# Low halves of part of the feed-forward weights formed by transfers that add the raw weight onto the negated high half

## The chip, the cores and the metric

The kernel runs on one core of one Trainium2 chip. The metric is the device time of one execution in microseconds. Engines are named as in the profile: PE multiplies matrices (PEld is its loading of weights), DVE is the vector engine, ACT the scalar engine, POOL the general-purpose one, and SP issues most transfers.

## The reference

The kernel computes a small encoder trunk for one sequence of 512 tokens with 1024 features, in float32. There are two layers, and each has four stages:

```
h = h + 0.5 * swiglu(rmsnorm(h, ffn1_norm[i]), ffn1_w_gu[i], ffn1_w_down[i])
h = h + mixer(rmsnorm(h, mix_norm[i]))       # layer 0: state-space scan, layer 1: neighbourhood attention
h = h + 0.5 * swiglu(rmsnorm(h, ffn2_norm[i]), ffn2_w_gu[i], ffn2_w_down[i])
h = h + sigmoid(rmsnorm(h, ple_norm[i]) @ ple_w_gate[i]) * rmsnorm(p[i] @ ple_w_proj[i], ple_post_norm[i])
```

`swiglu(x, w_gu, w_down)` splits `x @ w_gu` into a gate and an up half of 2816 columns each and returns `(silu(gate) * up) @ w_down`. The feed-forward stages are numbers 0, 2, 4 and 6 of the eight.

## The kernel before

**Two halves for every operand.** PE multiplies in a rounded 32-bit format, `float32r`. To come close to float32, each operand is split into a high half, rounded to that format, and a low half, the raw value minus the high half. A product takes three matmuls: high weight by high input, high weight by low input, low weight by high input (`gemm`, lines 282 to 292). Activations are split as they arise (`split`, line 314). Weights are split as they come in, by `split_raw` (line 228): ACT casts the raw tile into a tile `wh`, and DVE subtracts it from the raw tile into a tile `wl`.

**Units.** Weights come in units, tiles of 128 partitions by up to 1024 columns: eight blocks of 128 by 128 for a gate or an up row of tiles ("gu"), four or six blocks for a row of the down projection. The first units of a feed-forward stage, those before `chunks[0][1]`, are plain: 8 gate or up units in stages 2, 4 and 6, and 12 in stage 0. The rest of the gate and up projection is done in groups `p` of seven products instead of eight: `block(p, i)` multiplies a sum or difference of quarter matrices, in the order `TURN` (0, 3, 1, 5, 2, 4, 6). The tiles for the seven are made by DVE from four raw tiles (lines 252, 255, 257 and 263). Two of the four raw tiles lie in buffers `wr`, two in wide tiles `md`. Block 1 and block 5 share one tile: as soon as block 1 has been split, DVE overwrites it with block 5's values (line 263). `ffn_order` interleaves blocks with the down units ("dn") of the chunk before; after the last block come eight down units.

**The order around the split.** `plan` (line 152) lists everything that is to be prepared, in order: "u" a unit that is loaded and split, "g" four raw tiles taken as a group, "s" a sum of them, "o" a block whose tile is split. `prep_next` (line 238) does the next item of that list, and `top_up` (line 224) then issues loads from SP until three raw tiles in `wr` and two in `md` are waiting. `wr` has four buffers. `unit` (line 267) prepares until three units are ready and hands out the first. `wh` and `wl` have three buffers each, so the split of a unit waits until PE is done with the unit three places before it. The order within each engine's queue is that in which the code issues; a transfer waits in its issuing engine's queue until what it reads is written and what it overwrites is free.

**Around the stages.** `ffn` starts with the sum of squares for the norm (`SumSq`, line 335: squares on ACT, adds on POOL but for the last on DVE); while the first gate and up units run, DVE and ACT form the inputs for the blocks (`sums`, line 472). Results leave the accumulators through DVE and ACT: down products are added into `h` on DVE (line 599), block products by `whole` (line 535) on both. In the last down units of a stage, `Norm.prep` splits the new `h` and feeds POOL with squares to add. The first four units of stage 0 are loaded and split by hand (`begun`, lines 1437 to 1455), and `next(todo)` skips them in the list. POOL issues no transfer in this kernel.

Of the kernel before, what the change touches and what calls it, by code (L numbers as in the profile page):

```python
# [11 lines left out]
ALU = mybir.AluOpType  # L12
# [10 lines left out]
FIRST = ((0, 6), (6, 10), (10, 14), (14, 18), (18, 22))  # L23
OTHERS = ((0, 4), (4, 8), (8, 12), (12, 16), (16, 22))
# [28 lines left out]
def ffn_order(chunks):  # L53

    for f in range(chunks[0][1]):
        yield "plain", f
    yield "pair", 0, 0
    for c in range(1, len(chunks)):  # L60
        a, b = chunks[c]
        blocks = [(p, i) for p in range(a // 2, b // 2) for i in TURN]
        d = 2 if c == 1 else 0
        for n, (p, i) in enumerate(blocks):
            yield "block", p, i
            while d < KD and (d + 1) * len(blocks) <= KD * (n + 1):
                yield "down", c - 1, d
                d += 1
    yield "between",
    for d in range(KD):  # L70
        yield "down", len(chunks) - 1, d
# [3 lines left out]
def trunk(ctx, tc, A, out):  # L75
    nc = tc.nc
    v, s, g, te, sy = nc.vector, nc.scalar, nc.gpsimd, nc.tensor, nc.sync
# [13 lines left out]
    def nm(t):  # L91
        uid[0] += 1
        return f"{t}{uid[0]}"
# [55 lines left out]

    stop = A.get("stage", 4 * DEPTH)  # L150

    def plan():

        for i in range(stop):
            l, w = divmod(i, 4)
            if w in (0, 2):
                gu, gw, dn = [A[f"w_{x}{2 * l + w // 2}"] for x in ("gu", "gw", "dn")]
                chunks = FIRST if i == 0 else OTHERS  # L160
                plain = chunks[0][1]

                def ahead(p, i_):
                    if i_ == 0:
                        yield "g", [gw[p - plain // 2, x, y] for x, y in ((1, 0), (0, 0), (1, 1), (0, 1))]
                    yield "s", (p, i_)

                for what, *a in ffn_order(chunks):
                    if what == "plain":
                        for x in range(2):  # L170
                            yield "u", gu[a[0], x]
                            if 2 * a[0] + x == (6 if i == 0 else 3):
                                for n in range(3):
                                    yield from ahead(plain // 2, n)
                    elif what == "block":
                        yield "o", a
                        if a[1] in TURN[4:] and a[0] < NF // 2 - 1:
                            yield from ahead(a[0] + 1, TURN.index(a[1]) - 4)
                    elif what in ("down", "pair"):
                        b = chunks[a[0]]  # L180
                        for d in range(a[1], a[1] + 1 + (what == "pair")):
                            yield "u", dn[d, :, b[0] * P:b[1] * P]
                    elif w == 2:
                        for n in range(2):
                            yield "u", A["w_proj"][l, n]
            elif w == 3:
                for n in range(KD):
                    yield "u", A["w_gate"][l, n]
            elif l % 2 == 0:
                for n in range(65):  # L190
                    yield "u", A["w_in"][n]
                for x in range(2):
                    for d in range(KD):
                        yield "u", A["w_out"][d, :, x * 1024:(x + 1) * 1024]
            else:
                for n in range(24):
                    yield "u", A["w_qkv"][n]
                for d in range(KD):
                    yield "u", A["w_ao"][d]

    todo = list(plan())

    loads = [x for what, a in todo if what in "gu"
             for x in (zip(a, ("wr", "wr", "md", "md")) if what == "g" else [(a, "wr")])]
    todo = iter(todo)
    raws, ready, splits, group, blocks = [], [], [], [], {}
    waiting = {"wr": 0, "md": 0}

    def load_unit():
        src, tag = loads.pop(0)  # L210
        raw = wp.tile([P, 1024], F32, name=nm("wr"), tag="wr", bufs=4) if tag == "wr" else wide()
        n = src.shape[-1]
        sy.dma_start(out=raw[:, :n], in_=src)
        raws.append((raw, n, tag))
        waiting[tag] += 1

    def take():
        if not raws:
            load_unit()
        raw, n, tag = raws.pop(0)  # L220
        waiting[tag] -= 1
        return raw, n

    def top_up():
        while loads and waiting[loads[0][1]] < {"wr": 3, "md": 2}[loads[0][1]]:
            load_unit()

    def split_raw(raw, n):
        hi = wp.tile([P, 1024], F32R, name=nm("wh"), tag="wh", bufs=3)
        splits.append(s.copy(out=hi[:, :n], in_=raw[:, :n]))  # L230
        lo = wp.tile([P, 1024], F32R, name=nm("wl"), tag="wl", bufs=3)
        v.tensor_sub(out=lo[:, :n], in0=raw[:, :n], in1=hi[:, :n])  # L232
        ready.append((hi, lo))

    def wide():
        return md().rearrange("p a b -> p (a b)")

    def prep_next():
        item = next(todo, None)
        if item is None:  # L240
            return False
        what, a = item
        if what == "u":
            split_raw(*take())
        elif what == "g":
            group[:] = [take()[0] for _ in range(4)]
        elif what == "s":
            p, i = a
            a21, a11, a22, a12 = group
            if i == 0:  # L250
                blocks[p] = {0: a11, 2: a21, 3: wide(), 4: a12, 6: a22}
                v.tensor_add(out=blocks[p][3], in0=a21, in1=a22)
            elif i == 1:
                blocks[p][1] = blocks[p][5] = wide()
                v.tensor_sub(out=blocks[p][1], in0=blocks[p][3], in1=a11)
            else:
                v.tensor_sub(out=a21, in0=a11, in1=a21)
        else:
            p, i = a
            b = blocks[p]  # L260
            split_raw(b[i], 1024)
            if i == 1:
                v.tensor_sub(out=b[5], in0=b[4], in1=b[5])
        top_up()
        return True

    def unit(last=False):

        while (not last or not ready) and len(ready) < 3 and prep_next():
            pass  # L270
        return ready.pop(0)

    def ahead(norm):

        with tc.issue_after(norm.ss.last.ins):
            for _ in range(4):
                prep_next()
# [409 lines left out]
    def ssd(norm, nxt):  # L687
# [31 lines left out]
        for k in range(KD):  # L719
            t = t2()  # L720
            v.scalar_tensor_tensor(out=t, in0=hk[k], scalar=col(norm.gain + k), in1=R, op0=ALU.mult, op1=ALU.mult)
            xn.append(md(F32R))
            split(xn[k], t, None)
            if k == 5:
                prep_next()
# [709 lines left out]
    n = Norm(C_G1)  # L1435
# [57 lines left out]
    for i in range(stop):  # L1493
# [12 lines left out]
        n = m  # L1506
# [102 lines left out]
```

## Time and profile before

| | |
|---|---|
| median of three runs | 2292.43 us (2291.95 to 2293.34) |
| the profiled execution: its time | 2293.67 us |
| the profiled execution: its span, first to last instruction | 2291.9 us |
| granted TensorE clock | 0.999 |
| PE busy | 2273.0 us |
| DVE busy | 1847.5 us |
| ACT busy | 1287.3 us |
| POOL busy | 324.6 us |
| DMA packets | 281.57 MB |

The span leaves out what lies before the first and after the last instruction; here that is 1.8 us. A row of the groups gives line, engine, operation, output and inputs, shapes and count, then the busy time and the mean of one in ns, then the engine's idle time ahead of these instructions and what ended it. A row of the chain gives its start and length in microseconds. A row of the timeline gives start and length, then the instruction. A row of the waits gives the total, the count and the longest. A row of the transfers gives size and median from issue to landing.

### The profile page before, as it was taken

To read this page: it belongs to the slowest core of one execution; us is meant where nothing else is said; L and a number is where in the kernel's file an instruction comes from. 1 tells how busy PE (TensorE), PEld (TensorE's weight loads), DVE (VectorE), ACT (ScalarE), POOL (GpSimd) and SP (SyncE) were. 2 spreads that over 40 slices of the span, in tenths; PEclk is the share of its full clock that TensorE was granted. 3 is DMA by queue.
4 is the path that set the end of the run, shared out by engine and by line. 5 is a ranking of instruction groups with operands and counts; after the bars stand their busy time and mean duration, and the time that the engine had idled before them with its cause. 6 is when DMAs were issued, how large, how long until landed. Compare 5 with 4: busy or idle time off the path is not lost.

```text
span 2291.9 us, 33293 instructions
## 1 busy us (share of the span) xinstructions
PE 2273.0 (99%) x12458; PEld 1949.9 (85%) x12458; DVE 1847.5 (81%) x2729; ACT 1287.3 (56%) x2332; POOL 324.6 (14%) x261
## 2 busy tenths in 40 slices
PE   9999999999999999999999999999999999999999
PEld 7888888888888888888888878888877888888887
DVE  8878878888788959988885898888577859888866
ACT  6444445777677765544456554445546755444463
POOL 0000001345555641000003100000110010000020
PEclk9999999999999999999999999999999999999999
DMA  5323323444444643233223233232457732333232
GB/s 193 111 91 103 105 83 138 151 153 139 147 138 150 186 165 120 101 103 106 97 76 108 101 103 105 93 106 74 168 173 219 230 114 89 105 110 106 79 98 77
DMA packets 105090, 281.57 MB, mean 123 GB/s; under 512 B 13008, under 2 KB 13904, under 8 KB 104928
## 3 DMA queue, kind: packets, MB, share of 16 engines
q1 hardware_dynamic: 104640, 279.30, 37.0%
q8 instruction: 98, 1.61, 0.3%
q14 instruction: 64, 0.52, 0.1%
q10 hardware_dynamic: 288, 0.14, 0.0%
HBM read 259.70 MB, written 13.40 MB: 119 GB/s over the span
## 4 chain that ended last, share of the span: by engine, by line
PE 88%; DVE 8%; ACT 1%; issue 1%; DMA 1%; POOL 0%; SPq 0%; DVEq 0%; POOLq 0%; ACTq 0%
PE ps L518 29%; PE ps L287 18%; PE ps L291 18%; PE ps L290 17%; DVE wl L232 2%; PE ps L929 1%; PE ps L970 1%; DVE md L317 1%; PE ps L950 1%; PE ps L885 1%; PE ps L874 1%; PE ps L1367 1%; PE ps L1313 1%; PE ps L1356 0%; DVE t L790 0%
## 5 line engine op out<-in xcount | busy, mean ns | idle before, releaser
L287 PE MATMUL ps<-md,wh 128*128 128x512 f32 (+1 forms) x2032 | 797.6, 393 | 1.5 <-DVE t L790 1.5
L291 PE MATMUL ps<-md,wl 128*128 128x512 f32 (+1 forms) x2032 | 791.6, 390 | 3.7 <-DVE wl L232 3.7
L290 PE MATMUL ps<-md,wh 128*128 128x512 f32 (+1 forms) x2032 | 790.5, 389 | 0.8 <-DVE md L320 0.8
L230 ACT CAST wh<-wr 128x1024 fp32r<-128x1024 f32 (+2 forms) x395 | 352.3, 894 | 399.5 <-PE ps L290 181.0
L232 DVE TENSOR_TENSOR wl<-wr,wh 128x1024 fp32r<-128x1024 f32 (+2 forms) x395 | 417.4, 1059 | 115.3 <-ACT wh L230 113.3
L291 PEld LDWEIGHTS ps<-md,wl 128*128 128x128 f32 x2032 | 381.9, 188 | 86.1 <-DVE wl L232 4.8
L287 PEld LDWEIGHTS ps<-md,wh 128*128 128x128 f32 x2032 | 382.1, 188 | 78.1 <-ACT wh L230 2.1
L290 PEld LDWEIGHTS ps<-md,wh 128*128 128x128 f32 x2032 | 382.2, 188 | 74.8 <-DVE md L320 1.1
L518 PE MATMUL ps<-md,wh 128*128 128x256 f32 (+1 forms) x1610 | 366.4, 308 | 0.0
L518 PE MATMUL ps<-sc,wh 128*128 128x512 f32 (+1 forms) x1190 | 362.2, 357 | 0.4
L345 POOL TENSOR_TENSOR sq<-sq,sq 128x512 f32<-128x512 f32 x71 | 101.1, 1424 | 1627.9 <-ACT sq L341 642.2
L230 ACT CAST wh<-md 128x1024 fp32r<-128x1024 f32 x175 | 184.2, 1053 | 204.1 <-PE ps L518 170.0
L518 PEld LDWEIGHTS ps<-md,wh 128*128 128x128 f32 x1610 | 261.1, 189 | 20.1
L518 PE MATMUL ps<-md,wl 128*128 128x256 f32 x980 | 277.0, 283 | 1.1 <-DVE wl L232 1.1
L518 PE MATMUL ps<-sc,wl 128*128 128x256 f32 x980 | 276.4, 282 | 0.5 <-DVE wl L232 0.5
L232 DVE TENSOR_TENSOR wl<-md,wh 128x1024 fp32r<-128x1024 f32 x175 | 214.2, 1225 | 65.2 <-ACT wh L230 61.0
L518 PEld LDWEIGHTS ps<-sc,wh 128*128 128x128 f32 x1190 | 209.8, 188 | 35.7 <-DVE t L542 1.0
L518 PEld LDWEIGHTS ps<-sc,wl 128*128 128x128 f32 x980 | 184.9, 189 | 6.0 <-DVE wl L232 1.7
L518 PEld LDWEIGHTS ps<-md,wl 128*128 128x128 f32 x980 | 185.4, 189 | 2.9 <-DVE wl L232 2.9
L599 DVE SCALAR_TENSOR_TENSOR hs<-ps,hs 128x512 f32<-128x512 f32 x152 | 104.6, 688 | 72.8 <-PE ps L291 72.3
L790 DVE SCALAR_TENSOR_TENSOR t<-ps,ccw,t 128x510 f32<-128x510 f32 (+1 forms) x180 | 134.0, 745 | 10.7 <-ACT t L786 7.9
L542 DVE TENSOR_TENSOR t<-ps,t 128x256 f32<-128x256 f32 x280 | 116.4, 421 | 7.2 <-ACT t L541 5.0
(216 smaller groups left out, 2454.5 us busy)
## 6 DMA issues: line engine op xcount, KB each, us to landing
wr<-in_w_gw_dram SPq DMA_DIRECT2D x70, 512.0 KB, 3.2
md<-in_w_gw_dram SPq DMA_DIRECT2D x70, 512.0 KB, 3.6
wr<-in_w_in_dram SPq DMA_DIRECT2D x65, 512.0 KB, 3.3
wr<-in_w_dn_dram SPq DMA_DIRECT2D x128, 256.0 KB, 2.6
wr<-in_w_gu_dram SPq DMA_DIRECT2D x32, 512.0 KB, 3.4
hs<-crow SPq DMA_DIRECT2D x64, 256.0 KB, 3.6
wr<-in_w_dn_dram SPq DMA_DIRECT2D x32, 384.0 KB, 3.0
wr<-in_w_qkv_dram SPq DMA_DIRECT2D x24, 512.0 KB, 3.8
```

Of the source, the lines that this page charges most:

```text
L230: splits.append(s.copy(out=hi[:, :n], in_=raw[:, :n]))
L232: v.tensor_sub(out=lo[:, :n], in0=raw[:, :n], in1=hi[:, :n])
L287: m = te.matmul(out=pt, lhsT=hi[:, sl], rhs=part(xp, 0, cols), start=first and k == 0, stop=False)
L290: te.matmul(out=pt, lhsT=hi[:, sl], rhs=part(xp, 1, cols), start=False, stop=False)
L291: gemm.last = te.matmul(out=pt, lhsT=lo[:, sl], rhs=part(xp, 0, cols), start=False, stop=last and k == n - 1)
L317: split.low = v.tensor_sub(out=dst[:, 1, :], in0=src, in1=dst[:, 0, :])
L345: (v if fast else g).tensor_add(out=self.acc, in0=self.acc, in1=q)
L518: mm = lambda o, w, x, st, sp_: te.matmul(out=o, lhsT=w, rhs=x, start=opens and st, stop=sp_, skip_group_check=not opens)
L542: v.tensor_add(out=o, in0=pt[j][:, :HT], in1=o)
L599: v.scalar_tensor_tensor(out=h[d], in0=pt, scalar=0.5, in1=h[d], op0=ALU.mult, op1=ALU.add)
L790: v.scalar_tensor_tensor(out=a[:, lo:hi], in0=src[:, lo + o:hi + o], scalar=w(j), in1=a[:, lo:hi], op0=ALU.mult, op1=ALU.add)
L874: te.transpose(out=pt[:, cs(i)], in_=src[:, cs(c)], identity=ident)
```

## The change

The list of things to prepare is built stage by stage, so that the units of each feed-forward stage can be counted. In these stages the plain units, and from then on every second unit (the second, the fourth and so on), are marked. For a marked unit, ACT casts the high half as before, and then writes the negated high half into the tile `wl`; POOL then issues a transfer that reads the raw tile and adds it onto `wl`. DVE's subtraction is left out for these units. All other units are split as before.

```diff
-    todo = list(plan())
+    todo, by_dma = [], set()
+    for i in range(stop):
+        here = len(todo)
+        todo += plan([i])
+        if i % 2 == 0:
+            units = [n for n in range(here, len(todo)) if todo[n][0] in "uo"]
+            plain = 2 * (OTHERS if i else FIRST)[0][1]
+            by_dma.update(units[:plain] + units[plain + 1::2])
...
-    todo = iter(todo)
+    todo = ((n in by_dma, *item) for n, item in enumerate(todo))
...
-    def split_raw(raw, n):
+    def split_raw(raw, n, by_dma=False):
         hi = wp.tile([P, 1024], F32R, name=nm("wh"), tag="wh", bufs=3)
         splits.append(s.copy(out=hi[:, :n], in_=raw[:, :n]))
         lo = wp.tile([P, 1024], F32R, name=nm("wl"), tag="wl", bufs=3)
-        v.tensor_sub(out=lo[:, :n], in0=raw[:, :n], in1=hi[:, :n])
+        if by_dma:
+            s.mul(out=lo[:, :n], in_=hi[:, :n], mul=-1.0)
+            g.dma_start(out=lo[:, :n], in_=raw[:, :n], accum_op=ALU.add)
+        else:
+            v.tensor_sub(out=lo[:, :n], in0=raw[:, :n], in1=hi[:, :n])
         ready.append((hi, lo))
...
-        what, a = item
+        dma, what, a = item
         if what == "u":
-            split_raw(*take())
+            split_raw(*take(), dma)
...
-            split_raw(b[i], 1024)
+            split_raw(b[i], 1024, dma)
```

More of the change, by code (lines that the diff above doesn't have):

```diff
@@ L150, in trunk, with plan @@
     stop = A.get("stage", 4 * DEPTH)
-    def plan():
-        for i in range(stop):
+    def plan(stages):
+        for i in stages:
             l, w = divmod(i, 4)
```

## The prediction

> **What bounds the kernel now.** I read the page's totals first, then the chain, then the busy time in the stretches where most of the changed weights are used, then who waited for whom.
>
> ```profile
> span 2291.9 us, 33293 instructions
> PE 2273.0 (99%) x12458; PEld 1949.9 (85%) x12458; DVE 1847.5 (81%) x2729; ACT 1287.3 (56%) x2332; POOL 324.6 (14%) x261
> ...
> PE 88%; DVE 8%; ACT 1%; issue 1%; DMA 1%; POOL 0%; SPq 0%; DVEq 0%; POOLq 0%; ACTq 0%
> ```
>
> PE is without work for 2291.9 - 2273.0 = 18.9 us in all. The 8% of DVE in the chain is no reserve of that size: the chain follows DVE while PE still works off earlier units. The block-and-down part of each of the four feed-forward stages shows it more sharply:
>
> ```profile
> core 0: us, PE busy (x) PEld busy (x) DVE busy (x) ACT busy (x) POOL busy (x), PEclk, DMA share, GB/s
> 82.00:330.00 248.00, 248.00 (x1478) 220.32 (x1477) 195.91 (x268) 115.48 (x173) 0.00 (x0) 1.00 0.28 90
> 950.00:1195.00 245.00, 245.00 (x1480) 218.20 (x1479) 205.13 (x284) 116.94 (x178) 0.00 (x0) 1.00 0.29 98
> 1350.00:1590.00 240.00, 239.50 (x1444) 212.89 (x1443) 202.53 (x278) 115.95 (x175) 0.00 (x0) 1.00 0.29 95
> 1990.00:2230.00 240.00, 240.00 (x1394) 211.45 (x1393) 189.17 (x260) 124.91 (x191) 13.98 (x10) 1.00 0.30 96
> sum 973.00, PE 972.50 PEld 862.86 DVE 792.75 ACT 473.28 POOL 13.98; mean PE 243.13 PEld 215.71 DVE 198.19 ACT 118.32 POOL 3.49
> ```
>
> In 973 us PE idles 0.5 us. DVE is busy for 81% of that time and hides behind PE completely. What PE waited for the low halves is small in the whole run:
>
> ```profile
> PEld ps L291 <- DVE wl L232: 4.8, 3, 3.1
> PEld ps L518 <- DVE wl L232: 4.6, 12, 0.6
> ```
>
> So relieving DVE can bring at most 4.8 + 4.6 = 9.4 us. The question is what the longer way of making a low half does to PE.
>
> **How much cover there is.** `wh` and `wl` have three buffers each, and `unit()` prepares up to three units ahead. A unit's split can start when the unit three before it is finished, and must be done when the two units between are finished. The cover is the length of two units.
>
> ```profile
> 203.14 2.81 PE ps L518 x16
> 205.95 0.24 PE ps L287
> ...
> 208.74 5.69 PE ps L518 x40
> ```
>
> These rows of the chain run without a gap, and give the lengths: a block takes 2.81 us, a down unit over four blocks (twelve matmuls) 208.74 - 205.95 = 2.79, so the cover is **5.6 us**. A gate or up unit has 24 of the same matmuls, 5.58 us; its cover is 11.2. What uses it today:
>
> ```profile
> 203.00 1.05 ACT L230 CAST wh<-wr 128x1024 fp32r<-128x1024 f32 x1 [1.00 <-ACT t L554]
> ...
> 204.08 1.23 DVE L232 TENSOR_TENSOR wl<-wr,wh 128x1024 fp32r<-128x1024 f32 x1 [0.21 <-ACT wh L230]
> ```
>
> The cast starts at 203.00, as the preceding down unit ends, and the low half is there at 205.31: 2.3 of 5.6 us.
>
> **The change part by part.** Counting in program order, 235 low halves go the new way: 121 blocks, 64 down units of 512 columns, 16 of 768, 2 `w_proj` units, and 32 gate and up units; all but the last 32 alternate with units split by DVE.
>
> ```profile
> L230 ACT CAST wh<-wr 128x1024 fp32r<-128x1024 f32 x235 | 245.7, 1049 | 208.6 <-PE ps L290 119.9 <-PE ps L518 33.1 <-issue 27.5
> L230 ACT CAST wh<-md 128x1024 fp32r<-128x1024 f32 x175 | 184.2, 1053 | 204.1 <-PE ps L518 170.0 <-PE ps L290 13.0 <-DVE md L263 11.5
> L230 ACT CAST wh<-wr 128x512 fp32r<-128x512 f32 x128 | 79.8, 623 | 149.5 <-PE ps L518 66.3 <-PE ps L290 45.3 <-issue 32.7
> L230 ACT CAST wh<-wr 128x768 fp32r<-128x768 f32 x32 | 26.8, 837 | 41.4 <-issue 18.8 <-PE ps L290 15.8 <-PE ps L518 6.1
> ...
> L232 DVE TENSOR_TENSOR wl<-md,wh 128x1024 fp32r<-128x1024 f32 x175 | 214.2, 1225 | 65.2 <-ACT wh L230 61.0
> L232 DVE TENSOR_TENSOR wl<-wr,wh 128x512 fp32r<-128x512 f32 x128 | 87.4, 684 | 4.1 <-ACT wh L230 3.7
> L232 DVE TENSOR_TENSOR wl<-wr,wh 128x768 fp32r<-128x768 f32 x32 | 31.6, 990 | 16.7 <-ACT wh L230 16.4
> ```
>
> Removed from DVE: 155 x 1.225 + 64 x 0.684 + 16 x 0.990 = 250 us, nearly all behind a busy PE, so worth nothing by itself. Added to ACT: a multiplication of the same shape as the cast, which I price like it: 155 x 1.05 + 64 x 0.62 + 16 x 0.84 = 216 us. Of these some 182 fall on the alternating parts, where ACT would rise from 473 to 655 of 973 us; it stays unbound, and the copies queued behind a multiplication are late by at most 1.05 us, less than a unit. But both casts of a unit now stand one behind the other on the way to its low half.
>
> Then comes a transfer that POOL issues and that adds. The trace has neither kind. The nearest rows:
>
> ```profile
> wr<-in_w_gw_dram SPq DMA_DIRECT2D x70, 512.0 KB, 3.2
> md<-in_w_gw_dram SPq DMA_DIRECT2D x70, 512.0 KB, 3.6
> ...
> wr<-in_w_dn_dram SPq DMA_DIRECT2D x128, 256.0 KB, 2.6
> ...
> md<-md SPq DMA_DIRECT2D x8, 256.0 KB, 6.3
> ```
>
> ```profile
> L345 POOL TENSOR_TENSOR sq<-sq,sq x71: 1286/1302/2275, 339.9 to 2241.0; 128x512 f32<-128x512 f32 x71
> ```
>
> Lower end for a block (512 KB): the plain load, 3.2 us. Upper end: the slow row from SBUF to SBUF, 6.3 us for 256 KB, doubled: 12.6. I take the loads as the nearer rows, as they move whole rows of these very tiles: 3.4 us (between 3.2 and 3.6), plus one more stream of 512 KB, since the adding transfer reads its destination too. The step from 256 to 512 KB costs 3.4 - 2.6 = 0.8, so two such steps, 1.6. For POOL's issuing I take the 1.3 us of its median instruction, as an estimate. Together 6.3 us for a block, and 2.6 + 0.8 + 1.3 = 4.7 for a down unit of 512 columns.
>
> A block's low half then takes 1.05 + 1.05 + 0.05 for the hand-overs (the cast above ended at 204.05, DVE began at 204.08), so 2.15, + 6.3 = 8.45 us against 5.6: it is late by **2.85 us**. A down unit takes 0.62 + 0.62 + 0.05 + 4.7 = 6.0, late by 0.4. The 768-column units stand mostly among their like, with 8 us of cover. Gate and up units have 11.2 and are not late.
>
> How often is it paid? While PE waits for one late unit, the buffers of the unit behind it are free already, so the next unit by transfer starts that much earlier: of two late blocks in a row the second is on time, and a down unit after a late block always is. In the program's order the 121 blocks form 50 runs between down units, of 1 to 6 blocks; a run of r pays (r+1)/2, rounded down, which gives 16 + 19 + 19 + 19 = 73 times. 73 x 2.85 = **208 us**.
>
> Smaller edits. At block 1, DVE overwrites the very tile that the transfer reads (line 263):
>
> ```profile
> L263 DVE TENSOR_TENSOR md<-md,md 128x1024 f32<-128x1024 f32 x35 | 42.6, 1218 | 0.0
> ```
>
> Nine of these now wait for a transfer, with DVE's evacuations and the next low half queued behind; DVE is released as PE starts block 1, and has 1.22 + 0.84 + 1.23 = 3.3 us to do against the block's 2.81: about 0.5 x 9 = 5 us. The raw buffer comes free later too, and SP's loads queue behind it:
>
> ```profile
> 196.06 0.33 SPq L213 DMA_DIRECT2D wr<-in_w_dn_dram  x1
> ...
> 208.55 0.62 ACT L230 CAST wh<-wr 128x512 fp32r<-128x512 f32 x1 [1.30 <-PE ps L290]
> ```
>
> Counting loads and casts in order, these are one unit: landed at 198.7, it lay ready for 9.9 us, more than the 6 us by which a release moves; nothing. Past POOL's queue: it has nothing in three of the four stretches, and in the fourth ten adds, in the last down units; each can be held by one issue. Nothing. Against the 5 us stand some 5 of the 9.4 that PE waits for low halves today. The sum is 208; with the profiled execution's 2293.7 us it makes 2501.7, and as that lies 1.2 above the median of the runs, **2500**.
>
> One rule of the Trainium skill prices a transfer of this path: "DMA: Bandwidth & Descriptors", section "Anatomy of one DMA — SWDGE (gpsimd) path", fits about 2.0 us plus the bytes over 436 GB/s for transfers that GpSimd issues, without a word on adding ones. For 512 KB that is an estimated 3.2 us, beside the 3.2 to 3.6 of the loads here; by it the sum would be zero, which is the second rival below. No run here shows such a transfer yet.
>
> **The rivals.** *A, the forecast (0.62)*: the transfer takes 4.5 to 8 us for a block, late by 1.05 to 4.55, 73 times: 77 to 332 us, 2369 to 2624 us, which is its own range. *B, a far slower transfer (0.20)*: more than 8 us, because adding runs at a fraction of the copying rate, or because issuing is held up by DVE. For it speak the 6.3 us row above and this one:
>
> ```profile
> L982 DVE TENSOR_TENSOR sc<-sc,md x16: 693/1480/1516, 471.9 to 837.6; 128x512 f32<-128x512 f32 x16
> ```
>
> The same instruction takes 0.69 or 1.48 us, and the long ones run beside POOL's adds; DVE and POOL can get in each other's way, and DVE is 81% busy here. The Trainium skill ("SBUF — State Buffer", "Who interferes with whom") says the same of a DVE instruction with two SBUF inputs beside a POOL instruction that reads SBUF. At 10 us a block is late by 6.55: 478 us, 2770. Against it: SP's loads take their 3.2 to 3.6 us beside the same busy DVE, and POOL has nothing else to do in these stretches. *C, hidden (0.09)*: up to 5.6 - 2.15 = 3.45 us for a block nothing is late. The plain load of the same size speaks for it, the second stream and POOL's issue against: 2292. *D, faster (0.09)*, the other side: again at most 3.45 us, and DVE, free of 250 us, no longer lets PE wait where the gate and up units start; most of the 9.4 us: about 2285.
>
> **How the numbers follow.** This kernel's measurement can tell about 0.2% (4.6 us) from no change. Slower by more: A and B, 0.82; within: C, 0.09; faster: D, 0.09. The predicted time is A's, 2500. The range leaves out D and the upper half of B: 2290 (no lateness) to 2790 (a transfer of some 10.2 us).
>
> **What would show it.** Right: PE's busy share falls to about 91%, with gaps of some 3 us, 70 to 80 of them in the four stretches, ahead of block matmuls (L518) and released by a transfer into `wl`; few ahead of down units; hardly any in gate and up units; DVE down by about 250 us and ACT up by about 216; the transfers' median from issue to landing, POOL's issue included, near 6.3 and 4.7 us. B shows as 9 us and more, with gaps at gate and up units too. Wrong: block transfers under 3.45 us and a full PE (C, D); or gaps that end with DVE or with a load, which would put the loss on line 263 or on the raw buffers.

## The result and the profile after

The changed kernel takes 2538.68 us (median of four runs, 2532.43 to 2545.55), before 2292.89 us: a ratio of 1.1076 (95% interval 1.1062 to 1.109), 246 us slower. The profiled execution took 2532.43 us. In the changed kernel the lines have moved by 11: the matmuls of the blocks are L529, those of the other units L298, L301 and L302, line 263 is now L274. In `split_raw`, L237 is the cast, L240 the negation on ACT, L241 the transfer and L243 DVE's subtraction.

From the page of the changed kernel (totals, queues, chain, transfers):

```profile
span 2530.6 us, 33976 instructions
...
PE 2345.1 (93%) x12458; PEld 1970.4 (78%) x12458; DVE 1632.9 (65%) x2494; ACT 1480.8 (59%) x2567; POOL 527.6 (21%) x496
...
q0 software_dynamic: 33840, 104.35, 22.2%
...
PE 57%; DMA 19%; issue 17%; DVE 4%; ACT 2%; POOL 0%; SPq 0%; POOLq 0%; DVEq 0%; ACTq 0%
...
wl<-md POOLq DMA_DIRECT2D x83, 512.0 KB, 5.0
wl<-wr POOLq DMA_DIRECT2D x72, 512.0 KB, 4.7
...
wl<-wr POOLq DMA_DIRECT2D x64, 256.0 KB, 3.2
```

The 235 transfers are there (33840 packets on a queue of their own), and they now make 19% of the chain. A block's takes 4.7 to 5.0 us from issue to landing, a down unit's 3.2. PE is without work for 2530.6 - 2345.1 = 185.5 us, 166.6 more than before. Whom PE waited for, in the changed kernel (total, count, longest):

```profile
PE ps L529 <- DMA wl<-md: 94.3, 62, 3.0
PE ps L302 <- DMA wl<-wr: 55.1, 39, 5.1
PE ps L529 <- DMA wl<-wr: 12.4, 7, 2.6
PE ps L529 <- DVE t L553: 7.4, 4, 1.9
```

Transfers into `wl` end 108 waits of 161.8 us: 69 of them (106.7 us) at blocks, the 39 of L302 (55.1 us) at the other units. By the trace, 11 of these 39 (18.0 us) lie in the gate and up units at the stage starts, and nearly all others in down units. The first of the four stretches, from the busy times by window, and the timeline of one block by transfer in it:

```profile
82.00:330.00 248.00, 220.33 (x1233) 187.06 (x1232) 133.59 (x188) 125.89 (x179) 30.43 (x35) 0.98 0.58 146
```

```profile
104.74 1.05 ACT L237 CAST wh<-md 128x1024 fp32r<-128x1024 f32 x1 [1.35 <-PE ps L529]
105.82 1.06 ACT L240 ACTIVATE wl<-wh 128x1024 fp32r<-128x1024 f32 x1
...
107.29 0.87 POOL L241 DMA_DIRECT2D wl<-md  x1 [5.68 <-ACT wl L240]
```

PE worked 220.33 of 248 us, where it had worked all 248. After the cast and the negation end at 106.88, POOL begins 0.41 us later, and its issuing takes 0.87.

Weight loads come late too. Who waited for them, before and then in the changed kernel:

```profile
ACT wh L230 <- DMA wr<-in_w_gu_dram: 2.8, 3, 1.0
ACT wh L230 <- DMA wr<-in_w_dn_dram: 1.0, 2, 0.6
DVE md L252 <- DMA wr<-in_w_gw_dram: 0.3, 1, 0.3
```

```profile
DVE md L266 <- DMA wr<-in_w_gw_dram: 39.6, 23, 4.8
DVE md L263 <- DMA wr<-in_w_gw_dram: 33.7, 16, 7.0
ACT wh L237 <- DMA wr<-in_w_gu_dram: 32.2, 13, 5.6
ACT wh L237 <- DMA wr<-in_w_dn_dram: 11.9, 6, 3.0
DVE md L263 <- DMA md<-in_w_gw_dram: 9.2, 3, 4.9
```

That is 126.6 us instead of 4.1 for the weights of the feed-forward stages. These are waits of ACT and DVE, not of PE; how much of them reaches PE is a question for the experiments.

PE's busy time has also grown, by 2345.1 - 2273.0 = 72.1 us, with the same 12458 matmuls. The mean granted clock is 0.984 instead of 0.999: (1 - 0.984) x 2530.6 - (1 - 0.999) x 2291.9 = **38 us** went to a slower clock. Windows around a wait of 1.78 us (for DVE, as it happens), then PE's timeline there:

```profile
87.00:90.00 3.00, 1.47 (x10) 1.11 (x8) 3.00 (x5) 1.13 (x3) 0.86 (x1) 1.00 0.25 51
90.00:92.00 2.00, 1.76 (x6) 1.46 (x7) 1.66 (x3) 0.64 (x1) 0.00 (x0) 0.62 0.94 186
92.00:94.00 2.00, 2.00 (x9) 1.71 (x8) 0.00 (x0) 1.46 (x2) 0.10 (x1) 0.53 0.00 0
94.00:97.00 3.00, 3.00 (x26) 2.91 (x25) 0.00 (x0) 1.05 (x1) 0.76 (x1) 1.00 0.64 128
```

```profile
90.24 0.63 PE L529 MATMUL ps<-sc,wh 128*128 128x512 f32 x1 [1.78 <-DVE t L553]
...
94.00 0.40 PE L529 MATMUL ps<-sc,wh 128*128 128x512 f32 x1
```

After the wait the clock is at about half for some 3.4 us (the shortfalls of the second and third window together), and the same matmul takes 0.63 instead of 0.40 us.

### The profile page after: what moved, and what is told of

It is laid out like the page before. It is cut to its first block, busy times and chain, and to the rows that moved or that the text cites. A ratio compares the mean times of both kernels' runs of the same rounds, so it can differ in the third digit from the quotient of the medians.

```text
span 2530.6 us, 33976 instructions
## 1 busy us (share of the span) xinstructions
PE 2345.1 (93%) x12458; PEld 1970.4 (78%) x12458; DVE 1632.9 (65%) x2494; ACT 1480.8 (59%) x2567; POOL 527.6 (21%) x496
## 3 DMA queue, kind: packets, MB, share of 16 engines
q0 software_dynamic: 33840, 104.35, 22.2%
## 4 chain that ended last, share of the span: by engine, by line
PE 57%; DMA 19%; issue 17%; DVE 4%; ACT 2%; POOL 0%; SPq 0%; POOLq 0%; DVEq 0%; ACTq 0%
PE ps L529 14%; PE ps L302 13%; PE ps L301 13%; PE ps L298 13%; DMA wl<-md 8%; DMA wl<-wr 6%; DMA wr<-in_w_gu_dram 1%; DMA wr<-in_w_dn_dram 1%; DMA wr<-in_w_gw_dram 1%; PE ps L940 1%; PE ps L981 1%; DVE wl L243 1%; PE ps L896 1%; PE ps L961 1%; PE ps L885 1%
## 5 line engine op out<-in xcount | busy, mean ns | idle before, releaser
L302 PE MATMUL ps<-md,wl 128*128 128x512 f32 (+1 forms) x2032 | 802.8, 395 | 55.8 <-DMA wl<-wr 55.1
L298 PE MATMUL ps<-md,wh 128*128 128x512 f32 (+1 forms) x2032 | 804.4, 396 | 1.4 <-DVE t L801 1.3
L301 PE MATMUL ps<-md,wh 128*128 128x512 f32 (+1 forms) x2032 | 797.4, 392 | 0.8 <-DVE md L331 0.8
L237 ACT CAST wh<-wr 128x1024 fp32r<-128x1024 f32 (+2 forms) x395 | 351.6, 891 | 376.7 <-PE ps L301 217.0
L302 PEld LDWEIGHTS ps<-md,wl 128*128 128x128 f32 x2032 | 385.8, 190 | 155.9 <-DMA wl<-wr 74.1
L298 PEld LDWEIGHTS ps<-md,wh 128*128 128x128 f32 x2032 | 385.8, 190 | 79.2 <-ACT wh L237 4.1
L301 PEld LDWEIGHTS ps<-md,wh 128*128 128x128 f32 x2032 | 386.1, 190 | 75.4 <-DVE md L331 1.1
L529 PE MATMUL ps<-sc,wh 128*128 128x512 f32 (+1 forms) x1190 | 372.7, 364 | 7.4 <-DVE t L553 7.4
L529 PE MATMUL ps<-md,wh 128*128 128x256 f32 (+1 forms) x1610 | 375.8, 313 | 4.0 <-ACT wh L237 3.8
L529 PE MATMUL ps<-sc,wl 128*128 128x256 f32 x980 | 285.7, 292 | 70.6 <-DMA wl<-md 58.1
L237 ACT CAST wh<-md 128x1024 fp32r<-128x1024 f32 x175 | 183.7, 1050 | 265.5 <-PE ps L529 215.1
L243 DVE TENSOR_TENSOR wl<-wr,wh 128x1024 fp32r<-128x1024 f32 (+2 forms) x243 | 270.6, 1115 | 103.2 <-ACT wh L237 96.1
L529 PE MATMUL ps<-md,wl 128*128 128x256 f32 x980 | 283.7, 290 | 36.6 <-DMA wl<-md 36.2
L241 POOL DMA_DIRECT2D wl<-wr x152 | 132.3, 870 | 833.6 <-ACT wl L240 586.7
L529 PEld LDWEIGHTS ps<-md,wh 128*128 128x128 f32 x1610 | 267.2, 194 | 27.6 <-ACT wh L237 7.7
L529 PEld LDWEIGHTS ps<-sc,wl 128*128 128x128 f32 x980 | 190.7, 195 | 91.9 <-DMA wl<-md 71.2
L529 PEld LDWEIGHTS ps<-sc,wh 128*128 128x128 f32 x1190 | 215.6, 194 | 41.5 <-DVE t L553 8.8
L529 PEld LDWEIGHTS ps<-md,wl 128*128 128x128 f32 x980 | 190.0, 194 | 52.8 <-DMA wl<-md 48.8
L240 ACT ACTIVATE wl<-wh 128x1024 fp32r<-128x1024 f32 (+2 forms) x235 | 217.3, 926 | 3.2
L241 POOL DMA_DIRECT2D wl<-md x83 | 72.3, 871 | 527.4 <-ACT wl L240 255.5
```

Of the source, the lines that this page charges most:

```text
L240: s.mul(out=lo[:, :n], in_=hi[:, :n], mul=-1.0)
L241: g.dma_start(out=lo[:, :n], in_=raw[:, :n], accum_op=ALU.add)
L298: m = te.matmul(out=pt, lhsT=hi[:, sl], rhs=part(xp, 0, cols), start=first and k == 0, stop=False)
L301: te.matmul(out=pt, lhsT=hi[:, sl], rhs=part(xp, 1, cols), start=False, stop=False)
L302: gemm.last = te.matmul(out=pt, lhsT=lo[:, sl], rhs=part(xp, 0, cols), start=False, stop=last and k == n - 1)
L529: mm = lambda o, w, x, st, sp_: te.matmul(out=o, lhsT=w, rhs=x, start=opens and st, stop=sp_, skip_group_check=not opens)
```

## The experiments

Each run has its own time before, on the same chip: 2292 to 2295 us. The change itself spread over 13 us in four runs, so single runs are not read closer than that.

| run | what it does | us |
|---|---|---|
| the change | | 2538.68 |
| e1 | plain gate and up units only | 2317.34 (ratio 1.0114, 1.0097 to 1.013) |
| e10 | blocks only | 2466.88 |
| e12 | down units only | 2323.88 (ratio 1.0132, 1.0115 to 1.0149) |
| e7 | transfer copies, doesn't add | 2359.79 |
| e3 | negated half first | 2498.09 |
| e8 | four buffers, four ahead | 2411.30 |
| e11 | e3, e8 and five raw buffers | 2346.69 |
| e6 | five raw buffers | 2516.87 |
| e2 | second pass on ACT, DVE adds | 2305.56 |
| e4 | transfers beside, from the raw tiles | 2387.00 |
| e5 | transfers beside, from the masks | 2743.43 |

The theory is the prediction's: a low half by transfer comes later than its two units of cover, and PE waits for it. The main rival is that the transfers cost by what they hold up elsewhere: loads, raw buffers, POOL, ACT.

**Which units pay: e1, e10, e12.** The edit is the list of marked units; e10 and e12 differ in the letter.

```diff
-            by_dma.update(units[:plain] + units[plain + 1::2])
+            by_dma.update(units[:plain])                                               # e1
+            by_dma.update(n for n in units[plain + 1::2] if todo[n][0] == "o")         # e10
+            by_dma.update(n for n in units[plain + 1::2] if todo[n][0] == "u")         # e9, e12
```

e1 was expected:

> Only the plain gate and up units (32 of the 235) are split by transfer; the alternating ones go back to DVE. Lateness theory (a low half by transfer takes about 8 us from the release of its buffers, and only units with less than that as cover are late): gate and up units have 11.2 us of cover, so no loss; between 2283 and 2297 us, likeliest 2290. Rival, every transfer costs wherever it stands (traffic, POOL, ACT): 32/235 of the 246 us, so about 2326.

It lost 25 us, nearer the rival's 34 than nothing, so the gate and up units are not free. Its waits and its queues at the start of stage 2 show why (waits; POOL's, then SP's timeline):

```profile
PE ps L302 <- DMA wl<-wr: 18.5, 10, 5.0
...
ACT wh L237 <- DMA wr<-in_w_gu_dram: 32.1, 15, 5.6
```

```profile
894.88 0.87 POOL L241 DMA_DIRECT2D wl<-wr  x1 [1.91 <-ACT wl L240]
...
903.13 0.33 SPq L220 DMA_DIRECT2D wr<-in_w_gu_dram  x1
```

The same load of before:

```profile
894.17 0.33 SPq L213 DMA_DIRECT2D wr<-in_w_gu_dram  x1
```

The raw buffer comes free only when the transfer has read it, and by the trace this one, issued at 894.88 beside several loads, landed 8.2 us later. So the load starts at 903.13 instead of 894.17, ACT waits for the raw weight, and its transfer starts late. Ten waits of PE follow. It is the chain of raw buffer, load, cast and transfer that is too long here, not the cover of `wl`: two of the four `wr` buffers are held by the raw tiles of the coming group.

> Of the alternating units only the 121 blocks are split by transfer; down, w_proj and plain units go back to DVE. Lateness theory: a block needs 1.05 + 1.05 + 0.4 + 4.9 = 7.4 us against 5.6, late by 1.8, for 73 to 121 blocks (fewer where one gives the next a head start), so 131 to 218 us and the slower clock after the long waits on top: 2425 to 2530. Rival, every transfer costs 1.05 us: 2420 at the most, and as much more than the run with the down units alone as 39 more transfers cost, 41 us.

The blocks alone cost 174 us, 1.44 each, within the theory's range.

> Of the alternating units only the down units (and the two w_proj units) are split by transfer, 82 in all; blocks and plain units go back to DVE. Lateness theory: a down unit of 512 columns needs 0.62 + 0.62 + 0.4 (hand-over to POOL) + 3.2 = 4.9 us against 5.6 of cover and is not late by itself: 2293 to 2315 us. Rival, every transfer costs about the same (246 us over 235, 1.05 each): 2375.

e9 gave 4584.86 us. In that execution every matmul was slow, in the stages without a changed unit too, with nothing for PE to wait for:

```profile
L298 PE MATMUL ps<-md,wh 128*128 128x512 f32 (+1 forms) x2032 | 1374.4, 677 | 0.0
```

The kernel before took 2292.64 us on the same chip. The run says nothing about the edit, and the same kernel was run again:

> The kernel of the run before that splits only the down and w_proj units by transfer, once more, since there every matmul of the whole run took twice its time (4584.86 us), in the stages without a changed unit too. Lateness theory as before: 2293 to 2315 us. Rival, every transfer costs about the same: 2375.

29 us for 82 transfers, 0.36 each: a little over the theory's range and far from one price for all. PE waited 20 times for a transfer:

```profile
PE ps L302 <- DMA wl<-wr: 20.9, 20, 2.6
```

The three parts, 25 + 174 + 29 = 228 of 246 us, nearly add up, and the blocks carry three quarters of it.

**The transfer's length: e7.**

```diff
-            g.dma_start(out=lo[:, :n], in_=raw[:, :n], accum_op=ALU.add)
+            g.dma_start(out=lo[:, :n].bitcast(F32), in_=raw[:, :n])
```

> The transfer copies the raw weight over wl and doesn't add, so the low halves are wrong; all waits, passes, buffers and places stay. If adding (a second stream to read) is what makes the transfer take 5 us for a block, it falls to about 3.9 and the 108 waits shrink by up to 1.1 us each: 2415 to 2460. If adding costs nothing beside copying, the transfer stays near 5 us and the time at 2525 to 2545.

It took 2359.79 us, 179 less than with adding: more than expected, because copying is faster than I had thought. Queues and transfers of e7:

```profile
q0 software_dynamic: 28720, 104.35, 11.1%
...
wl<-md POOLq DMA_DIRECT2D x83, 512.0 KB, 3.1
wl<-wr POOLq DMA_DIRECT2D x72, 512.0 KB, 2.9
wl<-wr POOLq DMA_DIRECT2D x64, 256.0 KB, 2.3
```

```profile
PE ps L529 <- DMA wl<-md: 24.0, 30, 2.2
PE ps L302 <- DMA wl<-wr: 12.1, 13, 2.6
...
PE ps L529 <- DMA wl<-wr: 0.6, 1, 0.6
```

Adding makes a block's transfer 1.8 to 1.9 us longer and doubles the share of the engines' time for the same bytes (22.2% against 11.1%). With copies, PE waits 44 times for 37 us. Only the transfer is different, and most of the loss goes with its length. But a shorter transfer also frees its raw tile sooner (ACT and DVE wait 51.4 us for weight loads instead of 126.6), so this run alone doesn't part PE's wait for the landing from the raw buffers; e8 and e6 do.

**The way and the cover: e3, e8, e11.** e3 makes the negated half first, straight from the raw weight:

```diff
-        splits.append(s.copy(out=hi[:, :n], in_=raw[:, :n]))
         lo = wp.tile([P, 1024], F32R, name=nm("wl"), tag="wl", bufs=3)
         if by_dma:
-            s.mul(out=lo[:, :n], in_=hi[:, :n], mul=-1.0)
+            s.mul(out=lo[:, :n], in_=raw[:, :n], mul=-1.0)
             g.dma_start(out=lo[:, :n], in_=raw[:, :n], accum_op=ALU.add)
-        else:
+        splits.append(s.copy(out=hi[:, :n], in_=raw[:, :n]))
+        if not by_dma:
```

> The negated high half is made first, straight from the raw weight, and the high half after it, so the transfer starts one ACT pass earlier (1.05 us for a block, 0.62 for a down unit of 512 columns); everything else, transfers and bytes and passes, is the same. Lateness theory: each of the 108 waits for a transfer is shorter by up to that; 80 to 110 us less than with the change, 2425 to 2460. Rivals, traffic or the raw buffers held longer or DVE stuck at the tile of block 5: 2520 to 2545, as with the change.

41 us less than the change's median: the right way, half the size. The waits for transfers are 81.9 + 33.4 + 20.7 = 136 us in 119 of them: shorter (1.14 us instead of 1.50), but not fewer. Waits:

```profile
PE ps L529 <- DMA wl<-md: 81.9, 67, 2.9
PE ps L302 <- DMA wl<-wr: 33.4, 38, 3.0
PE ps L529 <- DMA wl<-wr: 20.7, 14, 3.8
```

e8 changes `bufs=3` to `bufs=4` for `wh` and `wl`, `len(ready) < 3` to `< 4` in `unit`, and `md` to 22 buffers.

> The change with four buffers each for wh and wl, units prepared four ahead instead of three, and 22 md buffers to make room. The cover grows from two units (5.6 us) to three (8.4), against some 8.4 us from release to landing for a block. Lateness theory: most waits of PE for a transfer go, 2330 to 2410. Raw-buffer theory: four raw buffers can't feed it faster, 2470 or more.

2411.30, just above the theory's range: one unit more of cover takes 127 us off the change. The waits of ACT and DVE for weight loads didn't shrink with it (155.2 us, 126.6 in the change), so it is the cover that did this and not earlier loads. e11 adds e3 and a fifth `wr` buffer, with 21 for `md`:

> The change with four buffers each for wh and wl, units prepared four ahead, five raw buffers (21 md buffers to make room), and the negated half made first. From release to landing 1.05 + 0.4 + 4.9 = 6.4 us for a block, against 8.4 of cover: nothing late by itself. Lateness theory: 2300 to 2350 us, what is left is ACT's second pass and the starts of the stages. If something else in the change costs (POOL, traffic, the fewer md buffers), above 2380.

2346.69, within the range. Where nothing should be late any more, 28 blocks still are (and one other unit, by 0.3 us):

```profile
PE ps L529 <- DMA wl<-md: 28.6, 17, 3.0
PE ps L529 <- DMA wl<-wr: 14.1, 11, 3.1
```

Transfers differ: in the changed kernel the spread from issue to landing, over all 235, was

```profile
DMA to landing us min/median/max: 3.2/4.6/9.5
```

and in e11 it was 3.2/4.7/9.7. Of e11's 29 late transfers 15 had taken more than the 6.9 us that are left of its 8.4 us of cover after ACT's pass and the hand-over. Why the other 14 were late stays open.

**What the transfers hold up: e2, e4, e5, e6.** e2 keeps the second pass on ACT and lets DVE add:

```diff
-            g.dma_start(out=lo[:, :n], in_=raw[:, :n], accum_op=ALU.add)
+            v.tensor_add(out=lo[:, :n], in0=raw[:, :n], in1=lo[:, :n])
```

> The marked units keep the second pass on ACT (negated high half into wl), but DVE adds the raw weight instead of a transfer. Lateness theory: 1.05 + 1.05 + 1.23 = 3.4 us for a block, within the 5.6 us of cover: 2293, plus or minus 6. Rival, the second pass holds up ACT's other work (216 us more on ACT): most of the loss stays, above 2450.

2305.56, above the theory's range by 7 us and far from the rival's: the pass itself is not the cause, though it may cost some 10 us that I had put at nothing. In e4 and e5 the low halves come from DVE as before, and transfers add onto a tile that nobody reads, in e4 from the raw tiles, in e5 from a constant:

```diff
         if by_dma:
-            s.mul(out=lo[:, :n], in_=hi[:, :n], mul=-1.0)
-            g.dma_start(out=lo[:, :n], in_=raw[:, :n], accum_op=ALU.add)
+            g.dma_start(out=apart[:, :n], in_=raw[:, :n], accum_op=ALU.add)                                # e4
+            g.dma_start(out=apart[:, :min(n, M_N)], in_=msk[:, :min(n, M_N)], accum_op=ALU.add)            # e5
+            v.tensor_sub(out=lo[:, :n], in0=raw[:, :n], in1=hi[:, :n])
```

> The same 235 adding transfers read the same raw tiles, but add them onto a tile that nobody reads; the low halves come from DVE as before the change. One md buffer fewer (23 instead of 24) makes room for that tile, and ACT's second pass is left out. Traffic, POOL's work and the later release of the raw buffers stay, the wait of PE for the transfer goes. Lateness theory: 2293 to 2305. Rival, traffic and raw buffers held longer: most of the loss stays, above 2430.

e4 lost 94 us, between the two, though PE waited for no transfer. It overstates, as its transfers also wait for one another at their common tile, which holds the raw tiles longer:

```profile
POOL apart L242 <- DMA apart<-wr: 456.1, 105, 8.9
POOL apart L242 <- DMA apart<-md: 409.0, 78, 10.9
```

> As the run with the transfers beside (low halves from DVE, 235 adding transfers onto a tile that nobody reads, 23 md buffers), but the transfers read the constant masks (up to 896 columns) instead of the raw tiles, so no raw buffer waits for them. Raw-buffer theory (the loads come late because a raw tile is free only when the transfer has read it): 2290 to 2303 us, the 94 us of that run are gone. Traffic theory (transfers and loads get in each other's way): near that run's 2387, 2360 to 2390.

2743.43, as nobody expected, and as a whole it answers another question: transfers that wait for no weight queued up on POOL, one after another at their common tile, and POOL's other work stood behind them. Between the first stage and the second ACT waited 174.1 us for POOL's adds of squares, and PE once for 169.0 us for a cast behind that; in the state-space stage PE waited 118.9 us for POOL's line 914. But one stretch can be compared, the first of the four (windows of e4, then of e5):

```profile
82.00:330.00 248.00, 237.29 (x1350) 208.49 (x1350) 184.70 (x250) 104.44 (x157) 33.84 (x39) 0.97 0.66 163
```

```profile
82.00:330.00 248.00, 248.00 (x1474) 220.20 (x1473) 198.46 (x270) 114.50 (x171) 41.81 (x49) 1.00 0.72 166
```

With more transfers (POOL x49 against x39) and a higher DMA share, PE is full when the raw tiles aren't held, and loses 10.7 us when they are. Traffic and the missing `md` buffer cost nothing there; holding raw tiles does. How much of that is in the change itself, e6 was to say, with `bufs=5` for `wr` and 23 for `md`:

> The change as it is, with five raw buffers in place of four (and 23 md buffers). Raw-buffer theory: the part of the loss that comes from late loads shrinks, 2440 to 2495 us against 2532 to 2546 with the change. If only PE's wait for the landing counts, or traffic does: 2525 to 2545.

2516.87: about 20 us less, at the edge of what a single run tells, and short of the range. ACT and DVE now wait 71.6 us for weight loads instead of 126.6, and PE's waits for transfers hardly move (98.0 + 40.6 + 13.2 = 151.8 us instead of 161.8). It is e8 turned round: there the loads stayed late and the time fell by 127 us. So in the alternating parts PE waits first for the landing, and the raw buffer is a second, smaller limit. At the stage starts it weighs more: there the fifth buffer halves PE's waits, from 18.0 to some 9 us.

## Why the prediction was right, point by point

**Direction and time: right.** 2500 was forecast, 2538.68 came; the miss is 39 of 246 us. That it is so small is in good part luck: the sum had one term twice too large, and left out terms of about the same size. With the measured lengths its own working gives 73 x 1.8 = 131 us, little more than half of what was lost.

**The cover of two units, and PE with nothing to gain: right.** e7, e8 and e11 move the transfer's length and the cover, and the loss follows both. DVE's subtractions shrank by 417.4 + 214.2 - 270.6 - 112.5 = 248.5 us, as forecast (250), and nothing came of it. The negations on ACT took 217.3 us (216).

**The transfer's length: oversized.** 6.3 us was taken for a block, 4.7 to 5.0 came; 4.7 for a down unit, 3.2 came. In its terms, issuing took 0.87 instead of 1.3, and the second stream 1.9 instead of 1.6 (e7); what was too high is the base, as a copy takes 3.0 with the issuing in it. The rule of the Trainium skill ("DMA: Bandwidth & Descriptors", "Anatomy of one DMA — SWDGE (gpsimd) path"), an estimated 3.2 us for a block, agrees with e7's copies (2.9 to 3.1); for the adding transfers it is 1.5 to 1.8 us short.

**The hand-overs: undersized.** 0.41 us from ACT to POOL, where 0.05 was taken for both together. From release to landing a block needs 1.05 + 1.06 + 0.4 + 4.9 = 7.4 us; late by 1.8 and not 2.85.

**How often it is paid: about right for blocks, missing for the rest.** Of blocks 73 waits were forecast and 69 came, 1.5 us each, so 73 x 2.85 = 208 became 106.7 us. The rule behind the count holds only roughly: by the trace, 11 of the 69 blocks, and 4 of 27 late down units, came right after a late block. The other 39 waits, 55.1 us, are not in the sum at all, because two steps failed. Down units were priced at 0.4 us late and then counted nowhere (27 waits in the changed kernel; 20 in e12, with the `w_proj` units). Their median transfer of 3.2 us would be in time; the late ones of 512 columns had taken 4.5 us in the median, so it is the spread that is paid. And **"the raw buffer: nothing"** did not hold: that step compared one load's slack at one place with the delay of one release, and left out that two of four buffers are held by the group. ACT and DVE waited 126.6 us for weight loads instead of 4.1. With that step fell the one that gate and up units "are not late" (e1: 25 us).

**The clock: left out.** 38 us, through waits the sum had but priced only once. With the 161.8 us of waits these are 200 of the 238.7 us by which the span grew. The other 39 are 5 us of smaller waits and 34 us by which PE's busy time grew beyond that; what these 34 are is not shown, as the ends of matmuls are modelled.

**Line 263: at most as small as forecast.** DVE waited 3 times, for 3.5 us, for a transfer there (5 were put down); it was not taken out by itself.

```profile
  DVE md L274: 3.5, 3
```

**Rival B**, a far slower transfer, fell with the lengths; that DVE holds up POOL's issuing is not seen, as POOL's 235 issues took 0.87 us on average. **C and D** fell too, as a block's transfer was not under 3.45 us. e7 adds that even 3 us leave the kernel 65 us slower, so C's condition would not have been enough, and D's 9 us could not show.

## What to carry to other kernels

A buffer ring gives each producer a deadline: the time of the units between release and use. Moving one step of the producer from an idle-enough engine to a transfer lengthens the way by the transfer's whole latency plus every hand-over, and frees nothing if that engine was hidden. Then look one ring further back: what the slower step reads is held longer too, and that ring may have even less room. Size the cover by the slow transfers and not by the median: here they took twice as long.

## What the runs showed of the hardware that was not expected

An adding transfer within the on-chip memory takes 5.0 us for 512 KB where a copying one takes 3.0, and twice the engines' time.

Some short waits cost twice. A wait of 1.78 us, with PE busy for 1.47 of the 3 us from 87 to 90, was followed by some 3.4 us at half the clock. The Trainium skill ("TensorE: Matmul & The Clock Gate", "What's actually happening") describes a gate that halves the clock after an idle window of about 3.4 us and gives all of it back after a busy one of that length; the half and the length of the slow stretch agree with the rows above, but here no wait that long was needed. The trace's clock record has 21 slow stretches before the kernel's end, 18 of 3.4 us and 3 of 6.8, so most of the 108 waits were not followed by one. Ahead of each of the 21 PE had been busy for less than half of the 3.4 us before; five other such windows were followed by none, so the exact condition stays open.

In e9 the matmuls of L298 took 677 ns in the mean instead of 393 in e12, the same kernel, and PE was busy for 4577.4 instead of 2279.7 us, while the granted clock was recorded as 1.0. What slowed PE there stays open.
